# Weight tiles fetched in pairs, and a gather's activations fetched alongside the rows, in the PEER stage of a decoder trunk

## The chip, the cores and the metric

The kernel runs on one core of a Trainium2 chip. The metric is the device time of one execution in microseconds (us); of several runs the median counts. The core's engines work from instruction queues of their own and meet through semaphores: TensorE (PE, with its weight loads PEld), VectorE (DVE), ScalarE (ACT), GpSimd (POOL) and SyncE (SP, which here only issues DMAs).

## The reference

The reference is a trunk of two layers over 256 positions of 1024 numbers. Each layer has an attention mixer and then a PEER feed-forward part, each followed by a LayerNorm of `ALPHA * x + f(x)`. What the change touches is PEER: every position picks, for each of 8 heads, 16 of 128 x 128 experts by a product key, and adds up the experts' rows. In short:

```python
def peer(x, wq, sub, u, v):          # u, v: 16384 rows of 1024
    idx, gate = top experts of x for each of 8 heads (16 each) and the softmax of their scores
    act = gelu(sum(x[:, None, :] * u[idx], -1))       # [256, 128]
    return sum((gate * act)[:, :, None] * v[idx], 1)  # [256, 1024]
```

## The kernel before

The function `peer` (line 423) runs twice, once for each layer. It does not gather for most positions: it computes the product with all 16384 experts, and lets the weights of the experts that weren't chosen be zero. All 128 tiles of `u` (128 experts by 1024, 512 KB) go past first (the u stage) and give activations, kept in SBUF in the tiles A for the 192 first positions; then all 128 tiles of `v` (the v stage, the loop of line 820, step j). For the last 64 positions (`GT`) the activations go to a buffer in DRAM, `actD`, and the v stage does without zeros: 128 lists of (position, expert) pairs fit into 64 gathers of 128 rows of v each.

One step j of the v stage consists of

- the load of tile j of `p_v` by SP, far ahead (line 92),
- its split into two parts of fewer bits: `hi` by ScalarE (a cast, line 104), and `lo`, the rest, by VectorE (line 115). Both are held in four buffers each,
- the split of the weights A of this tile in the same way, into W (ScalarE line 746, VectorE line 751),
- 10 matmuls of 128 by 512 on TensorE (`acc`, line 181), which add tile j to both position halves: 6 for the first 128 positions and 4 for the others.

Beside it run the gathered rows of the last 64 positions. `g_row(c)` (line 453) is an indirect DMA of GpSimd that fetches 128 rows of `p_v`, 512 KB, into one of six buffers (`RING`). `g_act(c)` (line 457) is an indirect DMA of GpSimd that fetches 128 single activations, 4 bytes each, from `actD`; four of them fill a tile `gel`. `g_mac(c)` (lines 462 to 467, VectorE) multiplies row by weight and adds it into `gacc`; for every fourth c it first makes the weights `gw` of four from the tile `gel` (line 462). After its add it issues `g_row(c + 6)`. The 64 adds start at step 7 (`LEAD`) and come every 1.766 steps.

Weights are one long list, `stream`. `_sdma` issues loads in the list's order, up to the index that `_ahead` allows; it is called after each `lo`. A load goes into a place of the pool `sraw` (four buffers of one tile, `raw`). In the v stage there are four more places: the tile `spare` takes the buffer of the transposed input `hT`, which the u stage reads to its end (`more_raw`, line 128), so that eight tiles are on the way or in use. The first four tiles of v are loaded into `raw` while the u stage ends. A load into a place waits until VectorE has made the `lo` of the tile that was there. Nothing but the program's order and these semaphores sets the time of an instruction: the program is recorded in the order in which it is written.

The activations are fetched by this line, four in step 0 and then one in each step, up to step 60:

```python
for c in range(4) if j == 0 else range(j + 3, min(j + 4, 64)):
    g_act(c)
```

Of the kernel before, what the change touches and what calls it, by code (L numbers as in the profile page):

```python
# [12 lines left out]
F32 = mybir.dt.float32  # L13
# [11 lines left out]
P = 128  # L25
S = 256
D = 1024
# [8 lines left out]
GT = 64  # L36
ND = S - GT
RING, LEAD = 6, 7
GB = 0.8
GS = 2.0 ** 15  # L40


class Kern:
# [4 lines left out]

    def plan(self):
        I, L = self.I, []  # L50
        self.v0s, self.spare = [], None
        if "mla" in self.parts:
            L += [I["a_w_in"][k] for k in range(KC)]
            L += [I["a_wk"][i] for i in range(2)]
            L += [I["a_wq"][i] for i in range(3)]
            L += [I["a_wv"][i] for i in range(2)]
            L += [I["a_wq"][i] for i in range(3, 6)]
            L += [I["a_wo"][i] for i in range(KC)]
        for l in (0, 1):
            if l == 1 and "nsa" in self.parts:  # L60
                L += [I["s_wv"][i] for i in range(4)]
                L += [I["s_wT"][i] for i in range(4)]
                L += [I["b_wg"]]
                L += [I["s_wT"][i] for i in range(4, 8)]
                L += [I["b_wq"][i] for i in range(4)]
                L += [I["b_wq"][i] for i in range(4, 8)]
                L += [I["b_wo"][i] for i in range(KC)] + [I["b_wo"][i] for i in range(KC // 2)]
            if f"peer{l}" in self.parts:
                L += [I["p_wq"][l, i] for i in range(16)]
                L += [I["p_u"][l, (P - FIRST + j) % P] for j in range(P)]  # L70
                self.v0s.append(len(L))
                L += [I["p_v"][l, j] for j in range(P)]
        self.stream = L
        self.v0 = self.v0s[0]
        self.si = 0
        self.sd = 0
        self.sh = 0
        self.sl = 0
        self.raws, self.his, self.los = {}, {}, {}
        self.share = False  # L80
        self.alt = {}
        self.later, self.now = [], 0

    def _sdma(self, upto):
        while self.sd <= min(upto, len(self.stream) - 1):
            ap = self.stream[self.sd]
            n = ap.shape[-1]
            if self.spare is not None and self.v0 <= self.sd < self.v0 + P and (self.sd - self.v0) % 8 > 3:
                t = self.spare[:, (self.sd - self.v0) % 8 - 4]
            else:  # L90
                t = self.sraw.tile([P, n], F32, tag="raw", name="raw")
            self.nc.sync.dma_start(t, ap)
            self.raws[self.sd] = t
            self.sd += 1

    def _shi(self, upto):
        while self.sh <= min(upto, len(self.stream) - 1):
            i = self.sh
            self._sdma(i)
            if i in self.alt:  # L100
                self.his[i], self.los[i] = self.alt.pop(i)()
            else:
                self.his[i] = self.shl.tile([P, self.raws[i].shape[-1]], F32R, tag="hi", name="hi")
            self.nc.scalar.copy(self.his[i], self.raws[i])  # L104
            self.sh += 1
# [13 lines left out]
    def _ahead(self):  # L119

        n, v0 = self.sl + self.nraw - 1, self.v0
        if self.spare is not None:
            n = max(n, min(n + 4, v0 + P + 3))
        elif v0 - 4 < self.sl < v0 + P:
            n = min(n, v0 + 3)
        return n

    def more_raw(self):
# [199 lines left out]
    def build(self):  # L328
        tc, nc, I = self.tc, self.nc, self.I
        with ExitStack() as es:  # L330
            es.enter_context(tc.manual_schedule())
            pool = lambda *a, **k: es.enter_context(tc.tile_pool(*a, **k))
# [2 lines left out]
            self.small = pool(name="small", bufs=2)  # L335
            self.pr8 = pool(name="r8", bufs=2)
            self.nraw = 4
            self.sraw = pool(name="sraw", bufs=self.nraw)
            self.shl = pool(name="shl", bufs=4)
            self.pacc = pool(name="pacc", bufs=2, space=PSUM)  # L340
            self.pmm = pool(name="pmm", bufs=4, space=PSUM)
# [81 lines left out]
    def peer(self, l):  # L423
        tc, nc, I = self.tc, self.nc, self.I
        self.v0 = self.v0s.pop(0)
        with ExitStack() as es:
            pool = lambda st, name: st.enter_context(tc.tile_pool(name=name, bufs=1, reuse_waits="tile"))
# [22 lines left out]
            def g_row(c):  # L450
                if c < P // 2:
                    t = grow[c] = gat.tile([P, D], F32, tag="row", name="row", bufs=RING)
                    nc.gpsimd.indirect_dma_start(out=t, out_offset=None, in_=gtable,  # L453
                                                 in_offset=bass.IndirectOffsetOnAxis(ap=gidx[:, 0, c:c + 1], axis=0))

            def g_act(c):
                nc.gpsimd.indirect_dma_start(out=gel[c // 4][:, c % 4:c % 4 + 1], out_offset=None, in_=gplaces,  # L457
                                             in_offset=bass.IndirectOffsetOnAxis(ap=gidx[:, 1, c:c + 1], axis=0))

            def g_mac(c):  # L460
                if c % 4 == 0:
                    nc.vector.tensor_tensor(gw[:, c:c + 4], gel[c // 4], ggate[:, c:c + 4], op=OP.mult)
                t = grow.pop(c)
                if c == 0:
                    nc.vector.tensor_scalar(gacc, t, gw[:, 0:1], None, op0=OP.mult)
                else:
                    nc.vector.scalar_tensor_tensor(gacc, t, gw[:, c:c + 1], gacc, op0=OP.mult, op1=OP.add)  # L467
                g_row(c + RING)
# [143 lines left out]
            def g_flush(n=1):  # L612
                if len(gq) < n:
                    return
                while gq:
                    t0, oi, gs = gq.popleft()
                    ps = self.acc(t0 // 4 % 2)
                    for q in range(4):
                        for w in range(2):
                            self.mm(ps[:, q * P:(q + 1) * P], oi[:, q // 2, :, q % 2], gs[w][:, q // 2, :, q % 2],  # L620
                                    w == 0, w == 1)
                    pv = ps.rearrange("p (t j) -> p j t", t=4)
                    k = done["a"]
                    for x, j0, n in A:
                        m = min(max(k, 0), n)
                        if m > 0:
                            y = x[:, 0:m, t0:t0 + 4]
                            nc.vector.scalar_tensor_tensor(y, pv[:, j0:j0 + m], 1.0 / GS, y, op0=OP.mult, op1=OP.mult)  # L628
                        if m < n:
                            nc.scalar.activation(x[:, m:n, t0:t0 + 4], pv[:, j0 + m:j0 + n], AF.Copy, scale=1.0 / GS)  # L630
                        k -= n
                    done["g"] = t0 + 4
# [128 lines left out]
            for j in range(P):  # L761
# [3 lines left out]
                g_flush(2)  # L765
                run_side(1.6 if len(A) == 1 else GB)
                if not side and len(A) == 1:
# [3 lines left out]
                    n = P - FIRST - NEXT  # L771
# [4 lines left out]
            while side or gq:  # L776
                g_flush()
                run_side(GB)
            u_fin(pu)
# [19 lines left out]
            rate, gc = (P - 8 - LEAD) / 64, 0  # L799
# [20 lines left out]
            for j in range(P):  # L820
                if j == P - FIRST:

                    es_1.close()
                    late.append(es.enter_context(tc.tile_pool(name="late", bufs=2 * NT - 6, reuse_waits="tile")))
                    for q in range(P - NT, P - 3):
                        self.alt[self.si + q - j] = lambda: [late[0].tile([P, D], F32R, tag="keep", name="keep") for _ in range(2)]
                hi, lo = self.nxt(j < P - 2)
                w_lo(j + 2)
                w_hi(j + 3)
                if j == NEXT + 1:  # L830
                    hN = self.reload_h()
                if j + 4 == P - 1:
                    gb = self.load_gb(2 * l + 1)
                kept[j] = (hi, lo, WW.pop(j))
                for c in range(4) if j == 0 else range(j + 3, min(j + 4, 64)):
                    g_act(c)
                if late_sums:
                    late_sums.popleft()()
                while gc < 64 and j >= LEAD + int(rate * gc):
                    g_mac(gc)  # L840
                    gc += 1
                    if gc in (60, 64):
                        late_sums.append((g_alpha, g_copy)[gc == 64])
                v_mm(j, 0, (0, 1), j == 0, j == P - 1)
                if j < P - NT:
                    v_mm(j, 1, (0, 1), j == 0)
                    kept.pop(j)
# [785 lines left out]
```

## Time and profile before

| what | value |
|---|---|
| median of three runs | 1792.02 us (1788.25 to 1798.21) |
| the profiled execution | 1791.22 us |
| its span, first to last instruction | 1789.4 us |
| granted clock of TensorE | 0.992 |
| TensorE busy | 1730.8 us, 97% |
| VectorE busy | 1554.7 us, 87% |
| ScalarE busy | 1042.2 us, 58% |
| GpSimd busy | 494.5 us, 28% |

The page of the profile gives the span, the busy time of each engine, DMA queues and the costliest groups of instructions. The prediction uses four kinds of views beside it. The table by stretches gives, for each stretch of the span (us from its start), its length, then the busy time and the number (x) of instructions of PE, PEld, DVE, ACT and POOL, the granted clock, the mean busy share of the 16 DMA engines and GB/s. The groups of instructions give: line, engine, operation, out<-in, number | busy us, mean ns of one | idle time before them, with what ended it. The tables of waits give: who waited <- for what: us in all, times, the longest. In a timeline a row has a start, a duration, the engine, the line, the operation, out<-in, and in brackets the idle time before it and its releaser. "issue" and "remote" are releasers that the profile can't name: nothing that it shows was waited for.

### The profile page before, as it was taken

The numbers are of one execution on the slowest core, as the hardware profiler recorded it, in microseconds if no ns is written. First come the engines' busy times: TensorE is split into PE (matmuls) and PEld (weight loads), VectorE is DVE, ScalarE is ACT, GpSimd is POOL, SyncE is SP. The second block draws the span as 40 slices with busy tenths as digits, with TensorE's granted clock in tenths as the row PEclk, the third lists the DMA queues.
The fourth block names the chain that finished last, engine by engine and source line by source line (L and its number), as shares of the span: only waits on it lengthen the run. The fifth ranks groups of instructions, "written<-read, shape, count | busy, mean of one in ns | idle before, by whom it ended". The sixth has DMA issues, their size and how long they took to land. (4 is left out here: it accounts for less than half of the span.)

```text
span 1789.4 us, 30937 instructions
## 1 busy us (share of the span) xinstructions
PE 1730.8 (97%) x10610; PEld 1489.2 (83%) x10610; DVE 1554.7 (87%) x3675; ACT 1042.2 (58%) x2267; POOL 494.5 (28%) x441
## 2 busy tenths in 40 slices
PE   7999999999999999999897999999999999989997
PEld 6879999888888867888785789998888887768886
DVE  6778988989997989999768779988899987879998
ACT  6646455666666545556457755556666665445553
POOL 2110002000003777661431210020000007766630
PEclk9999999999999999999999999999999999999999
DMA  7445657555557999997671365666555558989992
GB/s 257 158 144 177 201 172 271 189 178 179 183 174 256 368 316 344 377 375 277 220 229 53 101 219 185 197 203 238 182 177 176 187 190 324 345 297 354 378 371 92
DMA packets 120654, 416.69 MB, mean 233 GB/s; under 512 B 18065, under 2 KB 20145, under 8 KB 119409
## 3 DMA queue, kind: packets, MB, share of 16 engines
q1 hardware_dynamic: 91008, 322.61, 53.6%
q0 software_dynamic: 29488, 92.10, 13.9%
q8 instruction: 84, 1.38, 0.3%
q14 instruction: 74, 0.60, 0.1%
HBM read 400.49 MB, written 13.63 MB: 231 GB/s over the span
## 5 line engine op out<-in xcount | busy, mean ns | idle before, releaser
L181 PE MATMUL mm<-hT,hi 128*128 128x256 f32 (+1 forms) x3360 | 838.6, 330 | 0.0
L181 PE MATMUL mm<-hT,lo 128*128 128x256 f32 x2376 | 638.2, 281 | 1.1 <-DVE lo L115 1.0
L104 ACT CAST hi<-raw 128x1024 fp32r<-128x1024 f32 (+1 forms) x463 | 484.2, 1048 | 255.2 <-PE acc L181 87.3
L115 DVE TENSOR_TENSOR lo<-raw,hi 128x1024 fp32r<-128x1024 f32 (+1 forms) x459 | 559.1, 1221 | 44.0 <-ACT hi L104 32.6
L181 PEld LDWEIGHTS mm<-hT,hi 128*128 128x128 f32 x3360 | 552.2, 188 | 49.3 <-issue 1.2
L181 PEld LDWEIGHTS mm<-hT,lo 128*128 128x128 f32 x2376 | 448.3, 189 | 15.5 <-DVE lo L115 1.9
L181 PE MATMUL acc<-hi,W 128*128 128x512 f32 x1476 | 419.6, 392 | 6.3 <-issue 4.7
L181 PEld LDWEIGHTS acc<-hi,W 128*128 128x128 f32 x1476 | 276.8, 188 | 71.5 <-issue 11.7
L181 PE MATMUL acc<-lo,W 128*128 128x512 f32 x984 | 307.3, 393 | 7.1 <-issue 4.7
L453 POOL DMA_INDIRECT row<-p_v,gidx x128 | 220.8, 1725 | 132.8 <-DVE gacc L467 90.7
L735 POOL DMA_DIRECT2D actD<-gst x64 | 34.9, 546 | 794.5 <-ACT gst L733 794.5
L181 PEld LDWEIGHTS acc<-lo,W 128*128 128x128 f32 x984 | 183.3, 188 | 54.8 <-issue 10.2
L104 ACT CAST hi<-spare 128x1024 fp32r<-128x1024 f32 x126 | 132.3, 1050 | 139.9 <-PE acc L181 101.7
L115 DVE TENSOR_TENSOR lo<-spare,hi 128x1024 fp32r<-128x1024 f32 x126 | 153.7, 1220 | 26.7 <-issue 16.9
L457 POOL DMA_INDIRECT gel<-actD,gidx x128 | 148.1, 1157 | 51.5 <-issue 37.8
L467 DVE SCALAR_TENSOR_TENSOR gacc<-row,gw,gacc 128x1024 f32<-128x1024 f32 x126 | 161.3, 1280 | 1.1
L727 ACT ACTIVATE mm<-mm 128x192 f32<-128x192 f32 (+23 forms) x170 | 40.9, 241 | 122.5 <-DVE mm L725 122.5
L751 DVE TENSOR_TENSOR W<-A,W 128x128 fp32r<-128x128 f32 (+1 forms) x512 | 107.5, 251 | 1.8 <-ACT W L746 1.8
L746 ACT CAST W<-A 128x192 fp32r<-128x192 f32 x256 | 88.3, 346 | 0.0
L725 DVE TENSOR_TENSOR mm<-mm,half 128x256 f32<-128x256 f32 x174 | 74.4, 428 | 15.1 <-ACT half L724 14.7
L628 DVE SCALAR_TENSOR_TENSOR A<-acc,A 128x176 f32<-128x176 f32 (+16 forms) x268 | 55.9, 274 | 34.7 <-PE acc L181 31.7
L730 ACT ACTIVATE A<-mm 128x192 f32<-128x192 f32 (+23 forms) x244 | 67.7, 277 | 7.1 <-DVE mm L725 2.0
(275 smaller groups left out, 1755.1 us busy)
## 6 DMA issues: line engine op xcount, KB each, us to landing
raw<-p_u SPq DMA_DIRECT2D x256, 512.0 KB
raw<-p_v SPq DMA_DIRECT2D x128, 512.0 KB
spare<-p_v SPq DMA_DIRECT2D x128, 512.0 KB
raw<-p_wq SPq DMA_DIRECT2D x32, 512.0 KB
actD<-gst POOLq DMA_DIRECT2D x64, 128.0 KB
raw<-b_wo SPq DMA_DIRECT2D x12, 512.0 KB
raw<-a_wo SPq DMA_DIRECT2D x8, 512.0 KB
raw<-s_wT SPq DMA_DIRECT2D x8, 512.0 KB
```

The source lines that it names most:

```text
L104: self.nc.scalar.copy(self.his[i], self.raws[i])
L115: e.tensor_tensor(self.los[i], raw, self.his[i].bitcast(F32), op=OP.subtract)
L181: self.nc.tensor.matmul(out, a, b, start=start, stop=stop)
L453: nc.gpsimd.indirect_dma_start(out=t, out_offset=None, in_=gtable, in_offset=bass.IndirectOffsetOnAxis(ap=gidx[:, 0, c:c + 1], axis=0))
L457: nc.gpsimd.indirect_dma_start(out=gel[c // 4][:, c % 4:c % 4 + 1], out_offset=None, in_=gplaces, in_offset=bass.IndirectOffsetOnAxis(ap=g ...
L467: nc.vector.scalar_tensor_tensor(gacc, t, gw[:, c:c + 1], gacc, op0=OP.mult, op1=OP.add)
L628: nc.vector.scalar_tensor_tensor(y, pv[:, j0:j0 + m], 1.0 / GS, y, op0=OP.mult, op1=OP.mult)
L725: nc.vector.tensor_tensor(ps[:, 0:S], ps[:, 0:S], t, op=OP.add)
L727: nc.scalar.activation(ps[:, 0:n], ps[:, 0:n], AF.Gelu)
L730: nc.scalar.activation(y[:, n:ND], ps[:, n:ND], AF.Gelu)
L746: nc.scalar.copy(WW[j][:, 0:ND], slot(j))
L751: nc.vector.tensor_tensor(WW[j][:, o:o + c.stop - c.start], slot(j)[:, c], WW[j][:, c].bitcast(F32), op=OP.subtract)
```

## The change

Two things are changed in the v stage.

The weight tiles of v come in pairs: where the first of a pair is due, one DMA of 1 MB loads tiles j and j+1. It is issued only once the second is allowed too (unless a tile is wanted at once). For that the four places of `raw` are one tile `raw4` of four parts, and a load's place follows from its index (`place`). In layer 0 the pairs are (0, 1), (2, 3), up to (126, 127). In layer 1 the ring stands at an odd place when v begins: tile 0 comes alone, then (1, 2), (3, 4), up to (125, 126), and 127 alone; tile 3 goes into `spare` there, and no longer into the ring. The look-ahead at the stage's edges follows suit.

The activations are fetched in another order: two in each of the first six steps (`AHEAD` is 12), and from then on one just in front of each added row, for 12 rows later.

```diff
+AHEAD = 12
...
                 self.v0s.append(len(L))
+                o = (len(L) - self.v0s[0]) % 4
+                self.pairs.update((len(L) + j, I["p_v"][l, j:j + 2].rearrange("j i d -> i j d")) for j in range(o % 2, P - 1, 2))
                 L += [I["p_v"][l, j] for j in range(P)]
...
-    def _sdma(self, upto):
+    def place(self, i):
+
+        return (i - self.vb) % 4
+
+    def _sdma(self, upto, now=False):
+
         while self.sd <= min(upto, len(self.stream) - 1):
-            ap = self.stream[self.sd]
-            n = ap.shape[-1]
-            if self.spare is not None and self.v0 <= self.sd < self.v0 + P and (self.sd - self.v0) % 8 > 3:
-                t = self.spare[:, (self.sd - self.v0) % 8 - 4]
-            else:
-                t = self.sraw.tile([P, n], F32, tag="raw", name="raw")
+            i, ap = self.sd, self.stream[self.sd]
+            n, k, q = ap.shape[-1], self.place(i), i - self.v0
+            o = self.place(self.v0)
+            ring = self.spare if self.spare is not None and 0 <= q < P and (q + o) % 8 > 3 else self.raw4
+            if 0 <= q < P and i in self.pairs:
+                if i == upto and not now:
+                    return
+                t = ring[:, k:k + 2]
+                self.nc.sync.dma_start(t, self.pairs[i])
+                self.raws[i], self.raws[i + 1] = t[:, 0], t[:, 1]
+                self.sd += 2
+                continue
+            t = ring[:, k, 0:n]
             self.nc.sync.dma_start(t, ap)
-            self.raws[self.sd] = t
+            self.raws[i] = t
             self.sd += 1
...
         if self.spare is not None:
-            n = max(n, min(n + 4, v0 + P + 3))
+            n = max(n, min(n + 4, v0 + P + 3 - self.place(v0)))
         elif v0 - 4 < self.sl < v0 + P:
-            n = min(n, v0 + 3)
+            n = min(n, v0 + 3 - self.place(v0))
...
-                for c in range(4) if j == 0 else range(j + 3, min(j + 4, 64)):
+                for c in range(2 * j, 2 * j + 2) if j < AHEAD // 2 else ():
                     g_act(c)
...
                 while gc < 64 and j >= LEAD + int(rate * gc):
+                    if gc + AHEAD < 64:
+                        g_act(gc + AHEAD)
                     g_mac(gc)
```

On TensorE, ScalarE and VectorE the instructions stand in the same order as before. GpSimd's queue in layer 0, some steps after the first added row, where `gel` with its number is the tile of four activations and `row` a gathered row; before:

```order
81 L457 DMA gel_1399<-actD,gidx 128x1
82 L453 DMA row<-p_v,gidx 128x1024
83 L457 DMA gel_1399<-actD,gidx 128x1 x2
84 L453 DMA row<-p_v,gidx 128x1024
85 L457 DMA gel_1400<-actD,gidx 128x1 x2
86 L453 DMA row<-p_v,gidx 128x1024
87 L457 DMA gel_1400<-actD,gidx 128x1 x2
88 L453 DMA row<-p_v,gidx 128x1024
```

and after the change:

```order
81 L468 DMA row<-p_v,gidx 128x1024
82 L472 DMA gel_1367<-actD,gidx 128x1
83 L468 DMA row<-p_v,gidx 128x1024
84 L472 DMA gel_1367<-actD,gidx 128x1
85 L468 DMA row<-p_v,gidx 128x1024
86 L472 DMA gel_1367<-actD,gidx 128x1
87 L468 DMA row<-p_v,gidx 128x1024
88 L472 DMA gel_1367<-actD,gidx 128x1
```

One and two activations by turns stood between two rows; now it is one each time, and this goes on until the 52nd added row, at about step 98, where the gathers of activations ended at step 60 before. SP's queue at the start of the v stage of layer 0, with the semaphores that each load waits for; before:

```order
178 L92 DMA raw<-p_v 128x1024 [waits DMAHW7_49,DVE_49,Activation_49]
179 L92 DMA raw<-p_v 128x1024 [waits DMAHW0_49,DVE_49,Activation_49]
180 L92 DMA raw<-p_v 128x1024 [waits DMAHW1_49,DVE_49,Activation_49]
181 L92 DMA raw<-p_v 128x1024 [waits DMAHW2_49,DVE_49,Activation_49]
182 L92 DMA spare<-p_v 128x1024 [waits PE_49]
183 L92 DMA spare<-p_v 128x1024 x3
```

and after the change:

```order
178 L102 DMA raw<-p_v 128x2x1024 [waits DMAHW0_49,DMAHW7_49,DVE_49,Activation_49]
179 L102 DMA raw<-p_v 128x2x1024 [waits DMAHW1_49,DMAHW2_49,DVE_49,Activation_49]
180 L102 DMA spare<-p_v 128x2x1024 [waits PE_49]
181 L102 DMA spare<-p_v 128x2x1024
```

Eight loads of one tile have become four of two, and each waits for the places of both its tiles.

More of the change, by code (lines that the diff above doesn't have):

```diff
@@ L50, in plan @@
         I, L = self.I, []
-        self.v0s, self.spare = [], None
+        self.v0s, self.spare, self.pairs = [], None, {}
         if "mla" in self.parts:
@@ L71, in plan @@
                 self.v0s.append(len(L))
+                o = (len(L) - self.v0s[0]) % 4
+                self.pairs.update((len(L) + j, I["p_v"][l, j:j + 2].rearrange("j i d -> i j d")) for j in range(o % 2, P - 1, 2))
                 L += [I["p_v"][l, j] for j in range(P)]
         self.stream = L
-        self.v0 = self.v0s[0]
+        self.v0 = self.vb = self.v0s[0]
         self.si = 0
@@ L98, in _shi @@
             i = self.sh
-            self._sdma(i)
+            self._sdma(i, True)
             if i in self.alt:
@@ L337, in build @@
             self.nraw = 4
-            self.sraw = pool(name="sraw", bufs=self.nraw)
+            self.raw4 = pool(name="sraw", bufs=1).tile([P, self.nraw, D], F32, name="raw")
             self.shl = pool(name="shl", bufs=4)
```

## The prediction

> **What bounds the kernel now.** I read the page first: which engine fills the span.
>
> ```profile
> span 1789.4 us, 30937 instructions
> PE 1730.8 (97%) x10610; PEld 1489.2 (83%) x10610; DVE 1554.7 (87%) x3675; ACT 1042.2 (58%) x2267; POOL 494.5 (28%) x441
> ```
>
> TensorE is the bound, and a change that leaves its work alone can only win back idle time or stretched matmuls. Where are those? The table by stretches cuts both v stages: from each stage's first activation gathers to the last ones (565 to 700, 1477 to 1628), and behind that, where rows are still gathered but activations no longer.
>
> ```profile
> core 0: us, PE busy (x) PEld busy (x) DVE busy (x) ACT busy (x) POOL busy (x), PEclk, DMA share, GB/s
> 565.00:700.00 135.00, 130.55 (x554) 102.30 (x553) 115.45 (x197) 70.52 (x112) 101.86 (x90) 1.00 0.94 341
> 700.00:820.00 120.00, 120.00 (x531) 99.34 (x531) 119.24 (x204) 69.09 (x106) 78.53 (x36) 1.00 0.99 373
> 1477.00:1628.00 151.00, 142.00 (x584) 109.09 (x583) 123.81 (x211) 74.51 (x117) 111.74 (x95) 0.98 0.91 321
> 1630.00:1735.00 105.00, 105.00 (x465) 86.95 (x464) 103.66 (x178) 60.70 (x93) 63.26 (x29) 1.00 1.00 374
> ```
>
> Without activation gathers a matmul takes 120/531 = 0.226 us, so one j (10 of them) 2.26 us. By that the first stretch holds 554 x 0.226 = 125.2 us of work in 135, the third 132.0 in 151: 9.8 + 19.0 = **28.8 us are lost**, all while activations are gathered, none behind them. That is the most the change can win. Finer pieces show when:
>
> ```profile
> 584.00:640.00 56.00, 56.00 (x247) 45.96 (x246) 52.92 (x92) 29.12 (x46) 44.31 (x40) 1.00 0.99 370
> 640.00:700.00 60.00, 55.55 (x225) 40.62 (x224) 48.41 (x81) 30.45 (x48) 42.95 (x39) 1.00 0.92 321
> 1490.00:1520.00 30.00, 27.03 (x107) 19.20 (x107) 24.44 (x42) 13.30 (x21) 23.23 (x21) 1.00 0.85 297
> 1600.00:1610.00 10.00, 6.49 (x15) 3.69 (x16) 5.26 (x8) 3.96 (x7) 4.41 (x5) 0.73 0.65 200
> ```
>
> In layer 0 the same density of gathers runs 56 us without loss, and then the loss comes. Something piles up. In layer 1 an early loss, 1490 to 1520, is 30 - 107 x 0.226 = 5.8 us; its neighbours in the timeline show a cause of its own:
>
> ```profile
> 1489.41 0.16 DVE L462 TENSOR_TENSOR gw<-gel,ggate 128x4 f32<-128x4 f32 x1 [5.13 <-DMA gel<-actD,gidx]
> 1503.69 1.05 ACT L104 CAST hi<-spare 128x1024 fp32r<-128x1024 f32 x1 [6.60 <-remote]
> ```
>
> VectorE stands 5.13 us before the first added row, because the first four activations haven't landed; with it the lo tiles of all later weights. Who waits otherwise is in the tables of waits: first of 1477 to 1630, then (the last two lines, the second from SP's own table) of 700 to 820.
>
> ```profile
> ACT hi L104 <- remote: 22.8, 7, 6.6
> DVE gw L462 <- DMA gel<-actD,gidx: 5.1, 1, 5.1
> ...
> ACT hi L104 <- PE acc L181: 48.2, 50, 1.0
> SPq L92 <- DVE W L751: 116.4, 55, 2.8
> ```
>
> In the quiet stretch the hi cast waits only for TensorE to free its buffer, 1 us a time. In the lossy one it waits up to 6.6 us for something the profile gives no name to. The DMA engines are not full just then (share 0.85 and 0.65 where the loss is largest, 0.99 where there is none), so it isn't bandwidth; what piles up is the gathers. GpSimd's groups, of 584 to 700 and then of 700 to 820:
>
> ```profile
> L457 POOL DMA_INDIRECT gel<-actD,gidx x49 | 56.6, 1155 | 14.9 <-issue 14.6 <-DMA row<-p_v,gidx 0.3
> L453 POOL DMA_INDIRECT row<-p_v,gidx x28 | 31.9, 1139 | 14.1 <-issue 5.3 <-DVE gacc L467 4.2 <-DMA row<-p_v,gidx 2.5
> ...
> L453 POOL DMA_INDIRECT row<-p_v,gidx x30 | 73.5, 2449 | 35.5 <-DVE gacc L467 33.9 <-issue 1.3 <-DVE lo L115 0.3
> ```
>
> Busy 56.6 + 31.9 and issue gaps 14.6 + 5.3 are 108 of 116 us: GpSimd issues gathers back to back, 77 in 116 us (0.66 per us). Behind, 34 in 120 us (0.28), and it waits for VectorE's added rows.
>
> **The change part by part.** *Activation gathers.* All 128 stay. Twelve come in the first six steps, at GpSimd's own pace as now (11 by step 7 before). Then one goes out per added row instead of one per j. An added row comes every 120/30 = 4.0 us, so two gathers per 4.0 us: 0.50 per us. Each pair of gathers needs 1.155 + 1.139 us and two gaps of 0.3: 2.9 of 4.0 us by the lossy stretch's prices, and GpSimd has pauses again. I take the late loss as gone: 28.8 - 5.8 = **-23.0 us** (ends 0 and -28.8; 640 to 700 speaks for loss at high density, 584 to 640 and 700 to 820 for none while nothing has piled up). The 5.8 stays: the first four activations leave in the same two steps. What is new: 104 gathers now lie beside steps 6 to 98, half of that stretch without loss today. Its nearest row by density (0.50 against 0.66 and 0.28) lies a little nearer the lossy one, but by GpSimd's need, 2.9 of 4.0 us, it doesn't saturate: **+3 us**, ends 0 (700 to 820) and +22.6 (each late gather keeps its price: 23.0 us over the 2 x 53 of now are 0.217 each, x 104). The added gather stands ahead of the row that waits for VectorE's add; no buffer has to come free for it, so it runs in that pause, and nothing on GpSimd waits behind it that isn't waiting anyway.
>
> *Pairs.* 256 loads become some 130 of twice the size. The number of transfer ends falls too. The DMA tables of 584 to 700, then of 700 to 820:
>
> ```profile
> DMA packets 12332, 39.97 MB, mean 345 GB/s; under 512 B 2727, under 2 KB 2727, under 8 KB 12194
> gel<-actD,gidx POOLq DMA_INDIRECT x49
> ...
> DMA packets 12439, 44.77 MB, mean 373 GB/s; under 512 B 1527, under 2 KB 1527, under 8 KB 12431
> spare<-p_v SPq DMA_DIRECT2D x28, 512.0 KB
> raw<-p_v SPq DMA_DIRECT2D x27, 512.0 KB
> row<-p_v,gidx POOLq DMA_INDIRECT x30
> ```
>
> Small packets: 2727/116 = 23.5 per us with loss, 1527/120 = 12.7 without; 1527 over its 91 transfers is 17 each. A gather more costs (2727 - 12.7 x 116)/45 = 28. After: 12.7 + 0.25 x 28 - 17 x 0.23 (half of 55 loads in 120 us) = 15.8 per us, much nearer the quiet stretch. So I let pairs add nothing of their own to the gain, but they help the +3 stay small.
>
> Their price is lateness. The first of a pair leaves one step later and lands with the second. From the timeline of the quiet stretch:
>
> ```profile
> 736.60 7.14 SPq L92 DMA_DIRECT2D spare<-p_v  x4
> 749.90 1.05 ACT L104 CAST hi<-spare 128x1024 fp32r<-128x1024 f32 x1 [0.96 <-PE acc L181]
> ```
>
> The first of these four has 749.90 - 736.60 = 13.3 us until its cast; the four go out within 7.14 us, 2.3 apart, so a pair, issued with its second, has 11.0 us. At 373 GB/s that carries 4.1 MB; the pair's 1 MB, 1.5 MB ahead of it and a gathered row are 3.0 MB or 8 us. It holds, by 3 us: **0** (below nothing: fewer waits of the cast for a landing are worth nothing where it waits for none; above: the ring's rival, below). TensorE's work hides it, and SP waits a step longer with nothing else queued behind it in this stage. Only layer 1's start is tight, where tile 3 moves from the ring of four, loaded early, into the spare place that is free only at the stage's start:
>
> ```profile
> 1468.46 1.75 SPq L92 DMA_DIRECT2D spare<-p_v  x4
> 1469.81 1.05 ACT L104 CAST hi<-raw 128x1024 fp32r<-128x1024 f32 x1
> 1472.19 1.05 ACT L104 CAST hi<-spare 128x1024 fp32r<-128x1024 f32 x1 [1.09 <-DMA spare<-p_v]
> ```
>
> The first spare tile landed 3.7 us after its issue; a pair at 1.4 us more (0.5 MB at 373 GB/s) lands at 1473.6, so the cast of tile 3 comes 3.8 us later than at 1469.81. TensorE comes to it three steps into the stage, 6.8 us behind its start: **+1 us**, ends 0 and +3.8.
>
> The Trainium skill (DMA: Bandwidth & Descriptors, section Bandwidth) has it that transfers should be batched to 1 MiB for three quarters of peak, which would speak for a gain from pairs everywhere. Here 0.5 MB loads already run beside the rows at 373 GB/s with a DMA share of 0.99 and TensorE waits for none, so by that rule too the sum stays.
>
> Sum: 1791.2 (the profiled execution) - 23.0 + 3 + 1 = **1772 us**. That execution lies 0.8 us under the median of 1792.0.
>
> **The rivals.** *The price stays with each gather.* If a gather hurts by itself (0.217 us) and not by density, 104 spread ones cost 22.6: 1791.2 - 23.0 + 22.6 + 1 = 1792 us. For it: the loss ends exactly with them. Against: 584 to 640. By a halfway law, in proportion to small packets above the quiet rate, (15.8 - 12.7)/(23.5 - 12.7) = 0.29 of today's 23.0 us in 224 us (584 to 700 and 1520 to 1628), over 2 x 92 x 2.26 = 416 us, 12 us remain: 1791.2 - 23.0 + 12.3 + 1 = 1782. The same Trainium skill page (section on the anatomy of one DMA) calls the semaphore write of a transfer's end essentially free; by that rule pairs lighten nothing, the rate is 19.7 per us, and the halfway law leaves 0.65 x 23.0 x 416/224 = 27.8 us: 1797. No row here prices a transfer's end alone.
>
> *The ring of pairs runs dry (slower).* A place is loaded, cast, freed and loaded again every 8 steps, 18.1 us. If a pair lands x us later than the 11.0 it has, the ring turns in 18.1 + x. For it: through step 98 the DMA engines would carry gathers on top of a share of 0.99, and 3 us are thin. From x = 0 on it decides: x = 1 for the 416 us costs 416/18.1 = 23 us, 1772 + 23 = 1795; x = 1.5 over 2 x 290 us of whole stages costs 48: 1820. Against: per us the bytes are those of the quiet stretch, where SP waits for a free place and not the cast for a load.
>
> *GpSimd is too slow (slower).* While VectorE is full (119.24 of 120) a row's issue takes 2.449 us. With a gather at 1.155 and two gaps it's 4.2 us against 4.0: rows fall 0.2 x 49 = 10 us behind, which six rows in front (24 us) absorb: nothing. If a gather then took 2.449 too, 5.5 against 4.0 gives 73 us, less some 16 of slack 57 per layer: 1886 us. Against: in 584 to 640 VectorE is 94% busy and 40 issues fit in 56 us. The Trainium skill (SBUF — State Buffer, two separate sides) states that VectorE's two-port operations lock GpSimd out of writing descriptors, which fits the 2449 ns; it's this rival's mechanism.
>
> *It doesn't do what it says.* The late loss has another cause, as the granted clock of 0.73 at 1600 to 1610 hints: then 1790 to 1792.
>
> **How the numbers follow.** Forecast 0.58 (own range 1763 to 1781), halfway law 0.09, price per gather 0.16, another cause 0.04, ring dry 0.08, GpSimd 0.05. A measurement can tell about 0.5% (9 us) from no change. Faster is forecast and halfway law: 0.67; same 0.20; slower 0.13. The range goes from all removed (1791.2 - 28.8 = 1762) to 1793, just past the price per gather, leaving the slower ones out.
>
> **What would show it.** Right: 640 to 700 and 1520 to 1628 at 2.26 us per j, GpSimd's issues in turn and pauses before rows, no unnamed wait of the hi cast above 1.5 us behind step 20, the 5 us before the first added row still there. Wrong: unnamed waits spread through step 98 (price per gather), waits of the hi cast for the DMA of a pair every second step (ring), VectorE waiting for rows (GpSimd), loss in the same places (another cause).

## The result

The changed kernel takes **1763.03 us** (median of four runs, 1759.84 to 1765.82) against 1792.08 before: a ratio of 0.9834, 95% interval 0.98 to 0.9868. It is 29 us faster. The forecast was 1772, with 1762 to 1793 as its range; the sign and the place were right, the gain was half as large again.

The profiled execution after the change took 1764.78 us. Its page begins:

```profile
span 1763.0 us, 30707 instructions
PE 1719.8 (98%) x10610; PEld 1493.1 (85%) x10610; DVE 1554.6 (88%) x3675; ACT 1043.3 (59%) x2267; POOL 486.9 (28%) x441
```

The counts of the five engines' instructions are the same as before, and the busy times of VectorE and ScalarE agree within 1.1 us. TensorE's busy time is 11 us shorter: matmuls in the lossy stretches were stretched (15 took 6.49 us from 1600 to 1610 before). The table by stretches, with the same cuts in layer 0, and in layer 1 two cuts that start with the v stage (it begins 9 us earlier than before there):

```profile
565.00:700.00 135.00, 135.00 (x598) 111.77 (x597) 129.56 (x223) 77.85 (x121) 103.07 (x78) 1.00 0.97 371
700.00:820.00 120.00, 120.00 (x531) 99.38 (x530) 116.58 (x197) 69.00 (x106) 68.86 (x48) 1.00 0.97 362
1460.00:1600.00 140.00, 139.40 (x612) 114.28 (x611) 128.99 (x225) 80.23 (x126) 101.48 (x75) 1.00 0.97 361
1600.00:1705.00 105.00, 105.00 (x465) 86.95 (x464) 103.25 (x177) 60.03 (x94) 74.55 (x49) 1.00 0.99 375
```

598 matmuls where 554 were, at full rate (0.226 us). The stretch from 700 on, which had 4 activation gathers before, now has them to about step 98, and holds its 531 matmuls as it did. In layer 1 most of what is lost lies in one piece, 1500 to 1510:

```profile
1490.00:1500.00 10.00, 10.00 (x46) 8.29 (x45) 8.12 (x14) 3.95 (x7) 7.87 (x9) 1.00 0.96 347
1500.00:1510.00 10.00, 9.46 (x41) 7.04 (x40) 8.58 (x15) 7.01 (x11) 5.02 (x6) 1.00 1.02 401
1510.00:1520.00 10.00, 10.00 (x46) 8.29 (x45) 9.96 (x19) 5.93 (x11) 8.48 (x6) 1.00 1.01 379
```

Where did the time go? TensorE's matmuls stand in the same order in both kernels, so the n-th of one can be set beside the n-th of the other. From the first to the last matmul that uses a tile of v, the two v stages took 300.1 and 309.0 us before and 290.4 and 291.5 after: 27.2 us less. The rest of the span agrees within 1 us.

The waits in 565 to 700 after the change, and in the last line one of 1450 to 1600. The unnamed waits of the hi cast ("remote": 13.5 us in layer 0 before, 22.8 in layer 1 with up to 6.6 each) are gone from layer 0; in layer 1 four are left, 5.8 us in all, and the longest of them is 3.1 us, at 1574, where the prediction wanted none above 1.5; TensorE loses nothing there. Some waits for a load have come, 8.5 us in layer 0, hidden by the tiles that TensorE has in front of it. GpSimd waits more for added rows than before (8.2 us in all against 4.2):

```profile
ACT hi L119 <- PE acc L196: 43.7, 44, 2.8
POOL row L468 <- DVE gacc L482: 8.2, 8, 1.2
ACT hi L119 <- DMA raw<-p_v: 4.9, 3, 2.3
ACT hi L119 <- issue: 4.8, 5, 1.0
ACT hi L119 <- DMA spare<-p_v: 3.6, 3, 1.8
DVE gw L477 <- DMA gel<-actD,gidx: 3.4, 1, 3.4
...
ACT hi L119 <- remote: 5.8, 4, 3.1
```

### The profile page after: what moved, and what is told of

Read it like the earlier page. It is cut to its first block, busy times and chain, and to the rows that moved or that the text cites. A ratio compares the mean times of both kernels' runs of the same rounds, so it can differ in the third digit from the quotient of the medians.

```text
span 1763.0 us, 30707 instructions
## 1 busy us (share of the span) xinstructions
PE 1719.8 (98%) x10610; PEld 1493.1 (85%) x10610; DVE 1554.6 (88%) x3675; ACT 1043.3 (59%) x2267; POOL 486.9 (28%) x441
## 4 chain that ended last, share of the span: by engine, by line
PE 88%; DVE 5%; DMA 3%; ACT 2%; issue 1%; POOL 0%; SPq 0%; ACTq 0%
PE mm L196 48%; PE acc L196 39%; PE mm L225 1%; DVE lo L130 1%; DMA raw<-p_wq 1%; ACT hi L119 1%; DMA actD<-gst 1%; DVE bnst L271 0%; DMA xT<-xT 0%; DMA raw<-s_wT 0%; POOL row L468 0%; DVE hN L293 0%; DVE hN L275 0%; DVE hN L268 0%; DMA spare<-p_v 0%
## 5 line engine op out<-in xcount | busy, mean ns | idle before, releaser
L196 PE MATMUL acc<-hi,W 128*128 128x512 f32 x1476 | 414.6, 389 | 0.3 <-ACT W L761 0.3
L196 PE MATMUL acc<-lo,W 128*128 128x512 f32 x984 | 303.3, 389 | 0.3 <-issue 0.3
L468 POOL DMA_INDIRECT row<-p_v,gidx x128 | 189.7, 1482 | 111.6 <-DVE gacc L482 63.8
L472 POOL DMA_INDIRECT gel<-actD,gidx x128 | 172.7, 1349 | 50.2 <-issue 37.8
```

Source lines behind the costliest of these rows:

```text
L196: self.nc.tensor.matmul(out, a, b, start=start, stop=stop)
```

## The experiments

Two questions: which of the two parts brought the gain, and what in the gathers stalls TensorE. Three theories of the first set: (A) GpSimd's gathers, packed tightly, are the cause, and pairs add nothing; (B) it is the sum of transfers' ends and small packets, to which loads add; (C) it is the number of loads.

**One part alone.** The first takes only the new order of the gathers, the second only the pairs:

```diff
 # new order alone: before, with
-for c in range(4) if j == 0 else range(j + 3, min(j + 4, 64)):
+for c in range(2 * j, 2 * j + 2) if j < AHEAD // 2 else ():
     g_act(c)
...
+    if gc + AHEAD < 64:
+        g_act(gc + AHEAD)
     g_mac(gc)
 # pairs alone: the changed kernel, with these lines undone
```

> Only the new order of the activation gathers (two in each of the first six steps, then one in front of each added row); weight tiles come one by one as before. Theory A (it is GpSimd's gathers back to back that stall the v stage): the whole gain is here, 1764 us. Theory B (it is the sum of transfer ends and small packets, to which the loads add): about half, 1772 to 1780. Theory C (it is the number of weight loads): no gain, 1791.

> Only the pairs of weight tiles; activation gathers in the old order, one in each step up to step 60. Theory A: no gain, 1791 to 1793 (the pairs' late start in layer 1 costs 1). Theory B: about half, 1772 to 1780. Theory C: the whole gain, 1764.

The new order alone takes 1776.18 us (ratio 0.9919, 0.9887 to 0.9951), the pairs alone 1782.33 (0.995, 0.993 to 0.997). Each brings a part, 16 and 10 us, and together 29. That speaks against A and C, and looks like B. But the places differ. The v stages took, in us (from the profiled executions; 290 is a stage without any loss):

| kernel | layer 0 | layer 1 |
|---|---|---|
| before | 300.1 | 309.0 |
| pairs alone | 300.1 | 300.9 |
| new order alone | 292.6 | 297.6 |
| both | 290.4 | 291.5 |

In layer 0 pairs alone bring nothing. In layer 1 they remove the early loss, and most of the later one stays: these are rows of pairs alone.

```profile
1490.00:1520.00 30.00, 30.00 (x134) 24.86 (x133) 29.93 (x52) 15.81 (x25) 23.40 (x23) 1.00 1.00 371
640.00:700.00 60.00, 58.23 (x253) 46.63 (x252) 54.54 (x94) 31.88 (x50) 45.76 (x40) 1.00 0.95 343
1520.00:1628.00 108.00, 102.49 (x432) 79.28 (x431) 92.11 (x157) 56.24 (x89) 76.83 (x67) 1.00 0.90 329
```

With the new order alone it is the other way round: the later loss is gone, the early one of layer 1 stays and grows, 100 matmuls in 30 us where 107 were:

```profile
1490.00:1520.00 30.00, 28.10 (x100) 19.58 (x99) 22.55 (x38) 12.63 (x20) 19.36 (x19) 0.89 0.81 285
640.00:700.00 60.00, 60.00 (x266) 49.67 (x265) 58.65 (x101) 34.24 (x54) 44.48 (x31) 1.00 0.99 373
1520.00:1628.00 108.00, 108.00 (x478) 89.41 (x478) 105.77 (x182) 62.00 (x95) 81.24 (x55) 1.00 0.99 373
```

**No activation gathers, or from SP.** The one leaves out the activation gathers, the other replaces each by a plain load that SP issues.

```diff
 # without activation gathers
-    g_act(c)
-    nc.vector.tensor_tensor(gw[:, c:c + 4], gel[c // 4], ggate[:, c:c + 4], op=OP.mult)
+    nc.vector.tensor_tensor(gw[:, c:c + 4], ggate[:, c:c + 4], ggate[:, c:c + 4], op=OP.mult)
 # loads by SP
 def g_act(c):
-    nc.gpsimd.indirect_dma_start(out=gel[c // 4][:, c % 4:c % 4 + 1], out_offset=None, in_=gplaces, ...)
+    nc.sync.dma_start(gel[c // 4][:, c % 4:c % 4 + 1], self.actD[:, c, 0:1])
```

> The kernel before without any gather of activations (left out: the gathered activations, so the weights of the gathered rows are made from the gates alone); the rows and single loads stay. Prices all 128 activation gathers. Theories A and B: 1762 to 1764, all 28.8 us of lost time in the v stages gone. Theory C: 1780 or more, since the loads are as many as before.

> The kernel before with each activation gather replaced by a plain load of 128 times 4 bytes from the same buffer, issued by SP at the same place of the program (left out: the list of indices, so the activations are those of one position). The same number of transfers and of small packets, but not GpSimd's. Theory A: 1764, since GpSimd then issues rows alone. Theory B: 1788 to 1795, since packets and transfer ends are as dense as before.

Both take what the changed kernel takes: 1763.28 us without gathers (ratio 0.9841, 0.9803 to 0.9879) and 1762.87 with SP's loads (0.9831, 0.9794 to 0.9869). So the activation gathers cost all of the 29 us before, and after the change at most the 1.6 us by which its v stages are longer. And theory B falls: SP's loads leave by far the most small packets of all. The DMA table of 584 to 700, with loads from SP:

```profile
DMA packets 19476, 43.94 MB, mean 379 GB/s; under 512 B 8904, under 2 KB 8904, under 8 KB 19338
```

8904 against 2727 before, and TensorE loses nothing. What hurts isn't what a gather moves, but how GpSimd makes it.

**What in a gather.** Next theories: (D) each gather costs by being issued by GpSimd, (E) by the elements of its list, (F) GpSimd hurts the others when it issues without a pause. Half of the elements; plain transfers from GpSimd; loads in halves; rows in halves, without activations:

```diff
 # half of the elements (the others are set to zero)
-    out=gel[c // 4][:, c % 4:c % 4 + 1] ... ap=gidx[:, 1, c:c + 1]
+    out=gel[c // 4][0:64, c % 4:c % 4 + 1] ... ap=gidx[0:64, 1, c:c + 1]
 # plain transfers
+    nc.gpsimd.dma_start(gel[c // 4][:, c % 4:c % 4 + 1], self.actD[:, c, 0:1])
 # loads in halves (tiles of v alone), with the new order of the gathers
-    self.nc.sync.dma_start(t, ap)
+    self.nc.sync.dma_start(t[:, 0:n // 2], ap[:, 0:n // 2])
+    self.nc.sync.dma_start(t[:, n // 2:], ap[:, n // 2:])
 # rows in halves
-    nc.gpsimd.indirect_dma_start(out=t, ..., in_=gtable, ...)
+    for q in (slice(0, D // 2), slice(D // 2, D)):
+        nc.gpsimd.indirect_dma_start(out=t[:, q], ..., in_=table of rows of 512, ...)
```

> The kernel before, each activation gather fetches 64 elements in place of 128 (left out: half of the activations, which are zero). As many gathers by GpSimd, half the elements. Theory D (each gather costs by being issued by GpSimd): no gain, 1788 to 1793. Theory E (the elements of its list cost): about half of the 29 us, 1775 to 1780. Theory F (what hurts is that GpSimd issues without a pause): between, by how much shorter an issue gets; with 1.1 us as before 1790, with half of it 1763.

> The kernel before, each activation gather replaced by a plain transfer of 128 times 4 bytes from the same buffer, still issued by GpSimd at the same place (left out: the list of indices). With SP as its issuer the same transfer cost nothing. Theory D: 1788 to 1793. Theory E: 1785 to 1793, 128 elements as before. Theory F: 1763 to 1768, since a plain issue takes GpSimd 0.55 us against 1.16 and leaves it pauses.

> The new order of the activation gathers with each weight tile of v loaded by two transfers of 256 KB (with one of 512 KB it is 1776, with half of one of 1 MB 1763). If the number of load transfers adds to the stall beside the gathers: 1795 to 1805. If pairs helped in another way (their bytes, the look-ahead, the waits of the cast): 1774 to 1780.

> The kernel before without activation gathers (1763), with each gather of 128 rows of 4 KB made two of 128 rows of 2 KB (left out: the gathered activations, and the rows are others). GpSimd issues 0.5 gathers per us through the whole v stage, as many as with the new order, of the same bytes as rows alone. Theories D and E (any gather counts): 1772 to 1785, as the new order with single loads or somewhat more. If only lists of single elements hurt: 1763. Theory F: 1763 to 1768.

Half of the elements gain nothing: 1796.45 us beside 1795.1 of the kernel before in these rounds (0.9998, 0.9976 to 1.002). E falls. Plain transfers by GpSimd, as many as before, take 1765.9 (0.9841, 0.9799 to 0.9883): D in its plain form falls, F or the lists are left. Rows in halves take 1770.33 (0.9874, 0.9829 to 0.9919): 0.5 gathers by list per us, a time between what the theories said. The profiled execution shows no loss in the v stages (290.4 and 289.9 us), but at 1765.79 it is the fastest of four that go up to 1775.45, so where the others lose their few us isn't known. Loads in halves take 1767.72 (0.9849, 0.9806 to 0.9891): better than whole tiles (1776.18), where the theory of the number of loads said 1795 or more. So neither more nor larger loads decide as such; the pairs' own part has another cause.

GpSimd's groups in 584 to 700 with half of the elements show why that gained nothing: an issue is as long as with 128.

```profile
L459 POOL DMA_INDIRECT gel<-actD,gidx x46 | 54.4, 1184 | 14.0 <-issue 13.7 <-DMA row<-p_v,gidx 0.3
```

**Lists, or GpSimd without a pause; and the start of layer 1.** Two plain transfers for each gather fill GpSimd as the lists do. The other runs change the start: one gather in each of the first seven steps, with single loads and with pairs; and, with single loads and twelve gathers in six steps, the first added row two steps later.

```diff
 # two plain transfers for a gather (x is another place)
+    nc.gpsimd.dma_start(gel[c // 4][:, c % 4:c % 4 + 1], self.actD[:, c, 0:1])
+    nc.gpsimd.dma_start(gel[x // 4][:, x % 4:x % 4 + 1], self.actD[:, x, 1:2])
 # gentle start
-AHEAD = 12
+AHEAD = 7
-for c in range(2 * j, 2 * j + 2) if j < AHEAD // 2 else ():
+for c in (j,) if j < AHEAD else ():
 # later first row (with AHEAD = 12)
-RING, LEAD = 6, 7
+RING, LEAD = 6, 9
```

> The kernel before with each activation gather replaced by two plain transfers of 128 times 4 bytes by GpSimd (left out: the lists, so the activations are those of one position). GpSimd is as full as before (2 x 0.57 us for 1.16), without lists. Theory F (GpSimd without pauses stalls the others): 1780 to 1795. If it is the gathers by list and their density: 1763 to 1767, and the semaphore records stay prompt.

> Single loads, activation gathers one in each of the first seven steps and then one in front of each added row (seven rows ahead instead of twelve): no row of thirteen gathers back to back at the start. With twelve in the first six steps it was 1776, and the loss lay at 1498 to 1510, early in layer 1. If the crowd of gathers at the start makes that loss: 1768 to 1771. If it's the wait of VectorE for the first four activations: 1774 to 1778, that wait stays at 5 us. If only pairs help: 1776.

> Single loads and the new order of gathers, with the first added row at step 9 in place of 7, so that VectorE no longer waits 5 us for the first four activations. If that wait makes the early loss in layer 1: 1768 to 1771. If the crowd of gathers does, or only pairs help: 1774 to 1778.

> The changed kernel with the gentle start of the gathers (one in each of the first seven steps, then one in front of each added row, seven ahead). At most 1.6 us are left to win in the v stages: 1761 to 1764 if the crowd at the start costs them, 1763 if not; slower, 1766 or more, if seven ahead is too few for VectorE not to wait.

Two plain transfers take 1784.37 us (0.9944, 0.9911 to 0.9977): a loss of 20 us comes back. But it isn't the same loss. Its waits in 1570 to 1650 have names:

```profile
DVE gacc L468 <- DMA row<-p_v,gidx: 17.3, 11, 2.9
PEld acc L181 <- DVE lo L115: 14.4, 10, 2.8
PE acc L181 <- DVE lo L115: 10.0, 8, 2.3
```

Here GpSimd is late with the rows, VectorE waits for them, its lo tiles come late and TensorE waits for those: the case "GpSimd is too slow" of the prediction. Before the change VectorE never waited for a row. And it comes later: in layer 0, where the kernel before lost 9.8 us up to step 60, this one holds the full rate with GpSimd as busy (86 us of 116; 56.6 + 31.9 before). Its row of 584 to 700:

```profile
584.00:700.00 116.00, 115.76 (x511) 95.56 (x509) 106.24 (x180) 66.87 (x104) 86.28 (x114) 1.00 0.97 346
```

So theory F falls for the loss before the change. To tell the two kinds of loss apart I also counted in the semaphore records of the traces, for all increments that instructions of TensorE, ScalarE and VectorE make, how many are recorded within 0.1 us of the instruction's modelled end (the rest comes later or has no record):

| kernel | 500 to 540 (u stage) | 584 to 700 | 720 to 800 |
|---|---|---|---|
| before | 1.00 | 0.40 | 1.00 |
| half of the elements | 1.00 | 0.52 | 0.97 |
| pairs alone | 1.00 | 0.51 | 1.00 |
| new order alone | 1.00 | 0.65 | 0.81 |
| loads in halves, new order | 1.00 | 0.59 | 0.81 |
| later first row, single loads | 1.00 | 0.66 | 0.71 |
| gentle start, single loads | 1.00 | 0.78 | 0.74 |
| gentle start, pairs | 1.00 | 0.80 | 0.82 |
| both | 1.00 | 0.82 | 0.92 |
| rows in halves, no activations | 1.00 | 0.90 | 0.91 |
| plain transfers, by GpSimd | 1.00 | 0.98 | 1.00 |
| two plain transfers | 1.00 | 0.97 | 0.98 |
| loads by SP | 1.00 | 0.97 | 0.99 |
| rows alone | 1.00 | 0.99 | 0.99 |

In 584 to 700 this goes by the number of gathers **by list** per us, not by how busy GpSimd is nor by packets: 0.62 to 0.66 gathers per us go with a count of 0.40 to 0.52, 0.50 to 0.56 with 0.59 to 0.90, and about 0.25 with 0.97 to 0.99. Where GpSimd is as full with plain transfers, the records stay prompt. At one density the loads count too: halves, whole tiles and pairs give 0.59, 0.65 and 0.82.

But the count says less than it seems to. Most of what isn't prompt has no record at all: of 358 increments in 584 to 700 before the change, 142 are recorded promptly and only 185 at any time. And a missing record is no late increment: with the new order alone, the hi casts that ended at 1497.75 and 1505.59 have no record, yet VectorE, which needs them, starts the `lo` of the same tiles at 1498.18 and 1505.99. Nor does the count give the loss: loads in halves have 0.59 and lose nothing in layer 0.

What shows late increments is an engine that waits. With the new order alone this can be followed one by one: ten matmuls that release a buffer ended from 1492.78, 1493.24 and on to 1505.59, and have ten records, at 1496.67, 1498.10, 1504.52 and 1505.91, and six within 0.3 us at 1508.81 to 1509.13. The hi cast, which waits for them, starts at 1496.70, 1504.54 and 1508.84:

```profile
1490.31 1.05 ACT L105 CAST hi<-spare 128x1024 fp32r<-128x1024 f32 x1 [0.96 <-PE acc L182]
1496.70 1.05 ACT L105 CAST hi<-spare 128x1024 fp32r<-128x1024 f32 x1 [5.08 <-PE acc L182]
1504.54 1.05 ACT L105 CAST hi<-spare 128x1024 fp32r<-128x1024 f32 x1 [6.54 <-PE acc L182]
1508.84 1.05 ACT L105 CAST hi<-raw 128x1024 fp32r<-128x1024 f32 x1 [3.00 <-remote]
```

By its cadence the second of these would have come at 1492.6. Four buffers of hi cover one such delay (9 us of matmuls), not two in a row.

The start: with single loads, the gentle start takes 1767.11 us (0.9836, 0.9792 to 0.988), the later first row 1767.14 (0.983, 0.9786 to 0.9875), against 1776.18 with neither. Both remove the early loss of layer 1. With the gentle start VectorE waits for the first activations just as long as before:

```profile
1482.15 0.17 DVE L463 TENSOR_TENSOR gw<-gel,ggate 128x4 f32<-128x4 f32 x1 [4.95 <-DMA gel<-actD,gidx]
```

So this wait alone doesn't make the early loss, as the prediction had it; it needs the crowd of 13 gathers beside it too, and either one taken away is enough. With the later first row the 13 still go out in a row, from 1474.4 to 1495.9, and it is the wait that is gone:

```profile
1485.98 0.16 DVE L463 TENSOR_TENSOR gw<-gel,ggate 128x4 f32<-128x4 f32 x1 [0.45 <-DMA gel<-actD,gidx]
```

Pairs with the gentle start take 1764.41 (0.9822, 0.9779 to 0.9866), as the changed kernel does. Against single loads with the same start that is 2.7 us for the pairs (1.4 in the v stages of the profiled executions), where with the crowd they are worth 13.

## Why the prediction was right, and where not

**The place and the sign: right.** The sum took 28.8 us as lost in the v stages, and kernels without the activation gathers show that these cost that much: 1763.28 us. TensorE was the bound, and nothing outside the v stages moved.

**"-23.0, the late loss is gone": right**, with the whole late loss gone in layer 0 and layer 1. The new order alone does it: its rows of 640 to 700 and 1520 to 1628 are at full rate, with as many gathers in all. The reason was half right. It is a matter of density. But GpSimd didn't get the pauses that the step worked out: at 1.155 + 1.139 us and two gaps it was to be busy 2.9 of 4.0 us. Its groups of 584 to 700 after the change:

```profile
L468 POOL DMA_INDIRECT row<-p_v,gidx x32 | 46.5, 1452 | 16.8 <-DVE gacc L482 8.2 <-issue 5.9 <-DVE lo L130 2.4
L472 POOL DMA_INDIRECT gel<-actD,gidx x33 | 42.9, 1301 | 10.1 <-issue 9.7 <-DMA row<-p_v,gidx 0.3
```

Issues got longer, and with their gaps GpSimd is taken 46.5 + 42.9 + 5.9 + 9.7 = 105 of 116 us. That is nearly the 108 of before, and TensorE loses nothing all the same. 65 gathers instead of 77 were enough; that gaps of GpSimd do it was not shown.

**"The 5.8 stays": wrong**, and the largest part of the miss. The step put the early loss of layer 1 down to VectorE's 5.13 us wait, since that row stood next to it. The step had a sign against it in its own trace: in layer 0 VectorE waited 3.2 us in the same place, and nothing was lost early. After the change the wait is 2.75 us in layer 1, and the loss some 1 us. The gentle start with single loads settles it: wait 4.95, and 0.6 us lost. Twelve gathers in the first six steps were taken to cost what eleven by step 7 did. With single loads they cost more: set beside the kernel without activation gathers, matmul by matmul, the new order alone falls 7.7 us back early in layer 1 and 2.2 early in layer 0, where the kernel before falls back 5.9 and nothing. The pairs take most of that away.

**"+3 for gathers where none were": too much**; 700 to 820 keeps 531 matmuls. **"+1 for the pairs' late start": the right sign, and less**; beside the kernel with single loads and no activation gathers, the n-th matmul falls 0.4 us back between 1440 and 1480, and 1.2 more up to 1520, where the piece 1500 to 1510 lies.

**"Pairs add nothing of their own": wrong**, by 13 us beside the crowded start; the argument by small packets behind it was wrong as well (8904 packets, no loss). That the pairs' lateness is hidden was right: the casts' waits for loads are 8.5 us in 565 to 700, all under cover. The rule of the Trainium skill on 1 MiB transfers (DMA: Bandwidth & Descriptors, section Bandwidth) changed nothing here, as the prediction took it: in 700 to 820 362 GB/s with pairs, 373 before. That the semaphore write of a transfer's end is essentially free (the Trainium skill, same page, section on the anatomy of one DMA) agrees with the halves: twice the ends, and 1767.72 against 1776.18.

**The rivals.** The price per gather fell: 104 late gathers cost nothing in their new order. The halfway law fell with the packets. GpSimd being too slow isn't what happened, but the two plain transfers show it to be real: VectorE waits for rows, and TensorE for VectorE. The ring of pairs never ran dry: six short waits for a load in 565 to 700, and TensorE at full rate. Another cause, the clock: it was 1.00 in layer 0's lossy stretch and in layer 1's early one, so it made neither loss. In layer 1 the trace before has one piece of 6.8 us at half clock, from 1604.7 on, and the new order alone has one from 1504.7 on; by itself each is worth at most 3.4 us.

The size: 1772 forecast, 1763.03 measured. Of the 9 us, 5 are the early loss and 3 the term for new gathers.

**What stays open.** Why gathers by list delay other engines' semaphore increments isn't shown; only that the list's length, packets, transfer ends and a busy GpSimd don't make it by themselves. That delays cause the loss is argued: it rests on their order in time, in one trace, and on the unnamed waits; no run here could delay an increment by itself. The prediction's "something piles up" isn't explained either: in layer 0 the loss begins at about step 35 before, but at step 10 with pairs alone and at 25 with half of the elements. How pairs lessen the early loss, and why halves are faster than whole tiles (they still lose 5 us early in layer 1, 295.0 us for that stage), isn't settled. And of the 13 us between the new order alone and both, the profiled executions show 8.3 in the v stages; the rest lies elsewhere, where the instructions are the same. The time between the two v stages alone was 608 to 615 us over all the traces, so differences of a few us between runs are no finding.

## What to carry to other kernels

Price an off-path engine not by its busy time alone: gathers by list that GpSimd issued back to back cost TensorE 29 us, while the DMA engines were not full where the loss was largest, and many of the waits had no name. When a wait has no name, look for what is issued at that time and not before or behind, and try it at a lower density or from another queue. And a row that stands beside a loss isn't its cause until one of them is taken away.

## What the runs showed of the hardware that I had not expected

- A gather of 64 elements by list takes GpSimd 1.184 us to issue, as long as one of 128 (1.155), and stalls TensorE just as much (1796.45 us). A plain transfer of the same 512 bytes takes GpSimd 0.57 us and stalls nothing (1765.9).
- Plain loads of 128 single numbers, issued by SP in a stretch that moved 379 GB/s in all, cost nothing measurable (1762.87 us against 1763.28 without them).
- With gathers by list at 0.66 per us only 40% of the engines' semaphore increments are recorded within 0.1 us of the instruction's end, and about half never (142 and 185 of 358); in the u stage, without gathers, all are. A missing record doesn't mean that an engine waited.
